# Column tiles of the input projection: split again at every use, or split once and reloaded as two parts

## The chip, the cores and the metric

The kernel runs on one core of a Trainium2 chip. The metric is the device time of one execution in microseconds (us), lower is better; given are the median and the extremes of three runs. A further execution was recorded by the hardware profiler; its own time stands beside its span in the table below. Engines are named as the profile names them: PE (TensorE; PEld its weight loads), DVE (VectorE), ACT (ScalarE), POOL (GpSimd), SP (SyncE, which here does nothing but issue DMAs).

## The reference, cut to what matters

One layer of a hybrid trunk over 2048 latent tokens (width 1024) and 256 context tokens, in float32:

- h = modulate(rmsnorm(x)); one projection p = h @ w_in, with w_in of 1024 x 3584. Its 28 column tiles of 128 are seven groups of four heads: forward gate (0 to 3), backward gate (4 to 7), v (8 to 11), q (12 to 15), output gate g (16 to 19), and u and v of a gated MLP (20 to 23, 24 to 27).
- The context uses the gates and v only (tiles 0 to 11), for the states in which the latent scans start.
- The first five groups feed a bidirectional gated linear recurrence with a 128 x 128 state per head; the last two feed a spatial gating unit over chunks of 128 positions.
- The outputs are joined and go through w_out, a residual add, a norm, a gated MLP with a 3x3 depthwise convolution, a residual add, and a last norm.

```python
q = split_heads(silu(p[..., 3*w:4*w]), HG_HEADS) * (HG_DIM ** -0.5)
o_f, h_f = chunk_gla(q, k_f, v, logf_f, h0_f)
o_b, h_b = chunk_gla(flip_t(q), flip_t(k_b), flip_t(v), flip_t(logf_b), h0_b)
```

## The kernel before, in words

**Products in three terms.** The operands go to TensorE in type f32r. A float32 operand a is split into hi = cast(a) and lo = a - hi, and a product is hi·hi + hi·lo + lo·hi. `split` (lines 117 to 120) issues the cast on ACT (L119) and the subtraction on DVE or POOL (L120). The transposed input is held as xh and xl, the context as ch and cl.

**The w_in stage.** The latent sequence is worked in two halves of 1024 tokens (hh = 0, 1), since xh and xl hold one half. A key is a column tile with a kind of input (context or latent). `run_banks` (L480 to L505) goes through a list of banks: 512 columns of the sequence (256 for the context), 24 matmuls each (8 slices of the contraction, three terms), after which a sink reads the PSUM bank. A latent key has two banks. In the first half the list mixes 12 context keys with 28 latent ones, in an order that is written out; the second half has 28 more, so there are 68 uses of 28 tiles. The two gate tiles of a head alternate bank by bank (forward, backward, forward, backward); otherwise a key's two banks follow each other.

**The column tiles.** `load_raw` (L199) loads a tile as 128 x 1024 float32 (512 KB, rows of 512 bytes in DRAM) into one of three raw buffers, which two background tasks share. `split_w` (L204) splits it into whi and wlo in one of two slots. `run_banks` splits the current key and the next one; a third is loaded ahead only around context keys. A slot is free when the last matmul of its old key is done; the cast waits for that. The subtraction runs on DVE for the first seven splits and then for the odd ones below 20, else on POOL.

**The recurrence.** `hg` (from L717) handles a head in steps: the sum of both keys (kd, L719, POOL), then seven levels. In each level TensorE makes score products (sc<-Q,K, eight chunks), DVE copies them by a mask (L745), multiplies the queries by totals of decay (`level_update`, L469), `level_keys` multiplies the keys, one half on DVE and the other on POOL (L544), with copies on ACT (L546), and `next_tot` (L471 to L477) makes the totals of the next level (L476). After the levels come transposes, state products, a chain and an output. In the second half `deferred` (from L819) finishes the first half's backward direction, with four loads.

**What sets the order.** The program is traced once. Steps of the recurrence (`hg_q`) and of background work (`bg_q`: x of the second half, the blocks of w_ada, w_out) are put between the matmuls of a bank by a running estimate of TensorE's time (`slot`); `later(fn, wait)` puts a function off by that many microseconds of the estimate. A scheduler then orders each engine's queue; instructions under `pin` keep the order of the trace. Each engine works its queue in order, SP too: an SP instruction that waits holds back all DMAs behind it.

**Other places the prediction names.** At the half turn, xh and xl are reloaded from DRAM in sixteen pieces of 512 KB (L992, L993). `w_out_ops` (L878 to L893) splits w_out in the first half and stores both parts in DRAM (wo_d, L891 and L892), from where 1 MB tiles are loaded at the end of the stage (L813). `x_start` loads, squares (L220) and transposes the first half of x beside the context keys. L639 is the gate product of the MLP heads on POOL (nt).

Of the kernel before, what the change touches and what calls it, by code (L numbers as in the profile page):

```python
# [9 lines left out]
F32 = mybir.dt.float32  # L10
F32R = mybir.dt.float32r
# [7 lines left out]
P = 128  # L19
D = 1024  # L20
NK = D // P
# [3 lines left out]
CTX = 256  # L25
# [8 lines left out]
AL = 512  # L34
# [38 lines left out]
def tile_trunk(ctx, tc, x, c, cx, c_ctx, w_ada, b_ada, norm_mix, norm_ffn, w_in, hg_norm, sgu_g, sgu_b,  # L73
               w_sp, b_sp, w_out, w_up, conv_w, conv_b, w_down, norm_final, masks, out):
    nc = tc.nc
    V, S, G, T = nc.vector, nc.scalar, nc.gpsimd, Tensor(nc.tensor)
    ld = nc.sync.dma_start
    st = nc.sync.dma_start
    pin = tc.keep_in_program_order
# [6 lines left out]
    dr = ctx.enter_context(tc.tile_pool(name="dr", bufs=1, space=DRAM))  # L86
# [30 lines left out]
    def split(hi, lo, raw, eng=None, keep=lambda i: i):  # L117

        keep(S.copy(hi, raw))  # L119
        (eng or G).tensor_sub(lo, raw, hi.bitcast(F32))  # L120
# [7 lines left out]
    class Pump:  # L128
# [22 lines left out]
        def slot(self):  # L151
            due = [fn for at, fn in self.soon if at <= T.t]
            self.soon = [e for e in self.soon if e[0] > T.t]
            for fn in due:
                fn()
            if self.tasks and T.t >= self.at:
                self.step()
# [11 lines left out]
    hg_q, bg_q = Pump(), Pump()  # L169
# [7 lines left out]
    with es1:  # L177
        ps = es1.enter_context(tc.tile_pool(name="ps1", bufs=1, space=PSUM, reuse_waits="tile"))
        p1 = es1.enter_context(tc.tile_pool(name="p1", bufs=1, reuse_waits="tile"))
# [11 lines left out]
        def bank(tag):  # L191
            return ps.tile([P, 512], F32, tag=tag, name=tag, bufs={"pj": 3, "sc": 2, "mi": 3}[tag])
# [1 line left out]
        def raw_tile():  # L194
            return p1.tile([P, D], F32, tag="raw", name="raw", bufs=3)

        w_n, w_raw, w_free = [0], {}, [0, 1]

        def load_raw(key):  # L199
            raw = raw_tile().rearrange("p (k c) -> p k c", c=P)  # L200
            ld(raw, w_in[:, key[0]:key[0] + P].rearrange("(k p) c -> p k c", p=P))
            w_raw[key] = raw

        def split_w(key, eng=None):  # L204
            if key not in w_raw:
                load_raw(key)
            raw, at = w_raw.pop(key), w_free.pop(0)
            hi = p1.tile([P, NK, P], F32R, tag=f"whi{at}", name="whi", align_bytes=AL)
            lo = p1.tile([P, NK, P], F32R, tag=f"wlo{at}", name="wlo", align_bytes=AL)
            w_n[0] += 1  # L210
            split(hi, lo, raw, eng or (V if w_n[0] < 8 or w_n[0] < 20 and w_n[0] % 2 else G))
            return hi, lo, at

        def x_sums():
# [30 lines left out]
        wts, rows, pa, nxt = {}, {}, {}, {}  # L245
# [53 lines left out]
        with tc.manual_schedule():  # L299
# [44 lines left out]
            for i in range(4):  # L344
                ld(xg[i], x_rows[i])
            ada_sums(6, 8)
            nxt[0, CTX] = split_w((0, CTX), G)
            ada_products(3, 1)
            pz = bank("pj")
# [6 lines left out]
            for k in range(4, NK):  # L356
                ctx_mod(k, V)
            nxt[HW, CTX] = split_w((HW, CTX), V)
        xl = p1.tile([P, NK, TH], F32R, tag="xl", name="xl", align_bytes=AL)
        xh = p1.tile([P, NK, TH], F32R, tag="xh", name="xh", align_bytes=AL)  # L360
# [110 lines left out]
        def next_tot(tot, W, B):  # L471
            nb = W // B
            od = B in (1, 4, 16, 64)
            t2 = ph.tile([P, 2 * (W // (2 if od else 4))], F32, tag=f"T{int(od)}", name="tot")
            t2 = t2[:, :nb].rearrange("p (d n) -> p d n", d=2)
            V.tensor_mul(t2, tot[:, :, 0::2], tot[:, :, 1::2])  # L476
            return t2  # L477


        def run_banks(banks, peek=None):  # L480

            keys = [(b[0], b[2]) for b in banks]
            tail = [(peek, 512)] if peek is not None else []
            for i, (col, n0, n, sink, pre) in enumerate(banks):
                if pre is not None:
                    pre()
                up = list(dict.fromkeys(keys[i:] + tail))
                for key in up[:2]:
                    if key not in nxt:
                        nxt[key] = split_w(key)  # L490
                if len(up) > 2 and up[2] not in w_raw and up[2] not in nxt and any(k[1] == CTX for k in up[:3]):
                    load_raw(up[2])
                hi, lo, at = nxt[keys[i]]
                hiT, loT = (chl, cll) if n == CTX else (xh, xl)
                pj = bank("pj")
                sl = slice(n0, n0 + n)
                for k in range(NK):
                    if k and n == 512:
                        slot()
                    T.matmul(pj[:, :n], hi[:, k, :], hiT[:, k, sl], start=(k == 0), stop=False)  # L500
                    T.matmul(pj[:, :n], hi[:, k, :], loT[:, k, sl], start=False, stop=False)
                    T.matmul(pj[:, :n], lo[:, k, :], hiT[:, k, sl], start=False, stop=(k == NK - 1))
                sink()(n0, n, pj[:, :n])
                slot()
                if keys[i] not in keys[i + 1:]:  # L505
                    w_free.append(nxt.pop(keys[i])[2])
# [57 lines left out]
        def ctx_state(h, F, K, vt):  # L564
            tot = F
            for B in LV:
                level_update(K, CTX, B, tot, True)
                tot = next_tot(tot, CTX, B)
            yield 9.5
            pt = bank("mi")  # L570
            for d in range(2):
                for i in range(2):
                    o = (2 * d + i) * P
                    T.transpose(pt[:, o:o + P], K[:, d, i * P:(i + 1) * P], ident)
            kt = ph.tile([P, 512], F32, tag="on", name="ckt", bufs=2)
            S.copy(kt, pt)
            yield 2.0
            pd = bank("mi")
            for d in range(2):
                for i in range(2):  # L580
                    o = (2 * d + i) * P
                    T.matmul(pd[:, o:o + P], kt[:, o:o + P], vt[:, i * P:(i + 1) * P], start=True, stop=True)
            for d, dst in ((0, hf[h]), (1, hb[h])):
                a, b = (0, 1) if d == 0 else (1, 0)
                t = ph.tile([P, P], F32, tag="cdh", name="cdh", bufs=2)
                S.copy(t, pd[:, (2 * d + a) * P:(2 * d + a + 1) * P])
                V.scalar_tensor_tensor(out=dst, in0=t, scalar=tot[:, 1 - d, b:b + 1],
                                       in1=pd[:, (2 * d + b) * P:(2 * d + b + 1) * P], op0=ALU.mult, op1=ALU.add)
            yield 0.0
# [19 lines left out]
        for h in range(NH):  # L609
            F, K, vt = sets[h % 2]  # L610

            def pre(h=h):
                if h >= 2:
                    need(hg_q, ("ctx", h - 2))
                if h:
                    F, K, vt = sets[(h - 1) % 2]
                    hg_q.add(marked(ctx_state(h - 1, F, K, vt), ("ctx", h - 1)))
# [99 lines left out]
        def hg(hh, h, F, K, qs, vt, sgt):  # L717
# [16 lines left out]
            for l, B in enumerate(LV):  # L734
                dims = [[2 * B, P // (2 * B)], [TH + B, 2], [1, B]]
                if B == 1:
                    dims = dims[:2]
                if B == P // 2:
                    dims = dims[1:]
                for g in range(0, NCH, 4):  # L740
                    pb = bank("sc")
                    for i in range(4):
                        off = (g + i) * P
                        T.matmul(pb[:, i * P:(i + 1) * P], K[:, 0, off:off + P], view(Q, off, dims), start=True, stop=True)
                    V.copy_predicated(sc[:, g:g + 4, :], view(msk, l * P, [[0, 4], [1, P]]),  # L745
                                      pb.rearrange("p (c t) -> p c t", t=P))
                level_update(Q, TH, B, tot, False)
                K = level_keys(K, B, tot)
                tot = next_tot(tot, TH, B)
                yield 4.2  # L750
# [227 lines left out]
        for item in "f1 v2 b1 f2 u2 b2 f3 v3 u3 b3".split():  # L978
# [8 lines left out]
            seq += with_post(part, post)  # L987
            post = nxt_post if item[0] == "b" else lambda: None
        run_banks(seq, 4 * HW)
        for q in range(0, TH, 512):  # L990
            for k in range(0, NK, 2):
# [37 lines left out]
        def wo_hook():  # L1029
# [3 lines left out]
            open_wo()  # L1033
        seq[i] = (*seq[i][:4], wo_hook)
        run_banks(seq)
        bg_q.drain()
        hg_q.flush()
# [29 lines left out]
    def c_tile():  # L1067
        return px.tile([P, NK, P], F32R, tag="fl", name="fl", bufs=2, align_bytes=AL)
# [50 lines left out]
    for n, u in enumerate(units):  # L1119
        at = first[n] if n < 2 else [14 * (n // 2) + 2 * i + 3 * (n % 2) for i in range(7)]  # L1120
# [307 lines left out]
    for n, (u, i) in enumerate(prods):  # L1428
# [5 lines left out]
        hi, lo = u.A[i]  # L1434
# [14 lines left out]
        if n == NP - 8:  # L1449
            g2.append(c_tile().rearrange("p a b -> p (a b)").bitcast(F32))  # L1450
            ld(g2[0], g_d[1:2, :].broadcast_to([P, D]))
            t = c_tile().rearrange("p a b -> p (a b)").bitcast(F32)
            for f in range(2):
                load_m(0, f, t[:, f * 512:f * 512 + 512])
        if n in (NP - 4, NP - 3, NP - 2):
            f = n - NP + 4
# [83 lines left out]
    for n in range(3, len(seq)):  # L1540
        tg, f = seq[n]
# [64 lines left out]
```

## Time and profile before

| | |
|---|---|
| time, median of 3 runs | 2584.08 us (2579.35 to 2584.96) |
| profiled execution, own time | 2583.23 us |
| its span | 2581.3 us |
| mean granted TensorE clock | 0.992 of full speed |
| w_in, raw loads | 68 of 512 KB |
| all DMA | 336.42 MB, mean 130 GB/s |
| HBM read, written | 236.69 MB, 97.59 MB |

The span runs from the first to the last instruction on record. A busy time is the time in which an engine had work; its share is that of the span. A row of a timeline gives start, duration, engine, line, operation, output <- inputs with shapes and, in brackets, how long the engine stood idle before it and what it then waited for. A group row gives the busy time of all, the mean of one in ns, and the idle time before them by releaser.

### The profile page before, as it was taken

The numbers are of one execution on the slowest core, as the hardware profiler recorded it, in microseconds if no ns is written. First come the engines' busy times: TensorE is split into PE (matmuls) and PEld (weight loads), VectorE is DVE, ScalarE is ACT, GpSimd is POOL, SyncE is SP. The second block draws the span as 40 slices with busy tenths as digits, with TensorE's granted clock in tenths as the row PEclk, the third lists the DMA queues.
The fourth block names the chain that finished last, engine by engine and source line by source line (L and its number), as shares of the span: only waits on it lengthen the run. The fifth ranks groups of instructions, "written<-read, shape, count | busy, mean of one in ns | idle before, by whom it ended". The sixth has DMA issues, their size and how long they took to land. (4 is left out here: it accounts for less than half of the span.)

```text
span 2581.3 us, 32786 instructions
## 1 busy us (share of the span) xinstructions
PE 2503.6 (97%) x12123; PEld 2066.2 (80%) x12123; DVE 1634.9 (63%) x2174; ACT 905.0 (35%) x1524; POOL 1052.7 (41%) x871
## 2 busy tenths in 40 slices
PE   7999999999999998999999999999999999999997
PEld 4787887888888887788788888788788888888886
DVE  5867784644555666466898778599999983212212
ACT  2554334333434332344433333333333332111111
POOL 1344232232243243002687887877877810000000
PEclk8999999999999999999999999999999999999999
DMA  8355445561022124668722222732222364313221
GB/s 286 105 193 163 145 123 196 184 209 58 30 86 82 43 84 163 212 208 273 243 88 95 77 92 89 268 125 90 88 89 89 101 204 128 114 45 114 73 90 67
DMA packets 282492, 336.42 MB, mean 130 GB/s; under 512 B 31057, under 2 KB 214089, under 8 KB 278621
## 3 DMA queue, kind: packets, MB, share of 16 engines
q1 hardware_dynamic: 279076, 333.59, 39.2%
q8 instruction: 96, 1.57, 0.2%
q10 hardware_dynamic: 3257, 0.75, 0.1%
q14 instruction: 63, 0.52, 0.1%
HBM read 236.69 MB, written 97.59 MB: 129 GB/s over the span
## 5 line engine op out<-in xcount | busy, mean ns | idle before, releaser
L1281 DVE SCALAR_TENSOR_TENSOR dn<-gp,taps,dn 128x1024 f32<-128x1024 f32 x352 | 448.0, 1279 | 20.6 <-ACT dn L1278 17.3
L120 POOL TENSOR_TENSOR Al<-raw,Ah 128x512 fp32r<-128x512 f32 x264 | 344.8, 1314 | 96.2 <-ACT Ah L119 88.4
L65 PE MATMUL pj<-xh,whi 128*128 128x512 f32 x896 | 364.9, 408 | 0.5 <-ACT xh L119 0.5
L65 PE MATMUL pj<-xl,whi 128*128 128x512 f32 x896 | 351.9, 393 | 1.8 <-DVE xl L120 1.1
L65 PE MATMUL pj<-xh,wlo 128*128 128x512 f32 x896 | 352.2, 393 | 1.0 <-DVE wlo L120 1.0
L65 PE MATMUL up<-xah,Al 128*128 128x512 f32 x704 | 275.8, 392 | 2.3 <-POOL Al L120 2.3
L65 PE MATMUL up<-xah,Ah 128*128 128x512 f32 x704 | 276.3, 393 | 1.7 <-ACT Ah L119 1.7
L65 PE MATMUL up<-yl,Ah 128*128 128x512 f32 x704 | 274.3, 390 | 3.2 <-DMA yl<-yd 3.1
L112 POOL TENSOR_SCALAR rs<-ss 128x1 f32<-128x1 f32 (+1 forms) x24 | 7.1, 297 | 642.0 <-DVE xt L1516 323.3
L119 ACT CAST Ah<-raw 128x512 fp32r<-128x512 f32 x265 | 161.1, 618 | 299.2 <-PE up L65 249.4
L120 DVE TENSOR_TENSOR ml<-mr,mh 128x512 fp32r<-128x512 f32 x85 | 58.7, 690 | 299.7 <-ACT mh L119 299.7
L120 POOL TENSOR_TENSOR wlo<-raw,whi 128x1024 fp32r<-128x1024 f32 x56 | 140.8, 2514 | 230.9 <-ACT whi L119 215.6
L65 PE MATMUL up<-yh,Ah 128*128 128x512 f32 x528 | 208.1, 395 | 0.0
L65 PE MATMUL up<-yh,Al 128*128 128x512 f32 x528 | 206.9, 392 | 0.0
L65 PE MATMUL up<-xal,Ah 128*128 128x512 f32 x528 | 205.5, 389 | 0.0
L65 PEld LDWEIGHTS pj<-xh,wlo 128*128 128x128 f32 x896 | 169.0, 189 | 37.3 <-DVE wlo L120 1.7
L65 PEld LDWEIGHTS pj<-xh,whi 128*128 128x128 f32 x896 | 169.6, 189 | 34.3 <-issue 3.5
L65 PEld LDWEIGHTS pj<-xl,whi 128*128 128x128 f32 x896 | 169.6, 189 | 33.5 <-DVE xl L120 2.1
L65 PE MATMUL dn<-wo,o 128*128 128x512 f32 x768 | 184.9, 397 | 3.7 <-DMA wo<-wo_d 2.2
L65 PE MATMUL dn<-wh,ml 128*128 128x512 f32 x480 | 186.8, 389 | 0.0
L65 PE MATMUL dn<-wl,mh 128*128 128x512 f32 x480 | 186.8, 389 | 0.0
L65 PE MATMUL dn<-wh,mh 128*128 128x512 f32 x480 | 186.7, 389 | 0.0
(307 smaller groups left out, 4941.2 us busy)
## 6 DMA issues: line engine op xcount, KB each, us to landing
raw<-in_w_up_dram SPq DMA_DIRECT2D x88, 512.0 KB
raw<-in_w_in_dram SPq DMA_DIRECT2D x68, 512.0 KB
mr<-m SPq DMA_DIRECT2D x85, 256.0 KB
raw<-in_w_ada_dram SPq DMA_DIRECT2D x32, 512.0 KB
m<-cv SPq DMA_DIRECT2D x22, 544.0 KB
m<-cv SPq DMA_DIRECT2D x22, 480.0 KB
xt<-in_w_down_dram SPq DMA_DIRECT2D x19, 512.0 KB
wa<-in_w_ada_dram SPq DMA_DIRECT2D x8, 1024.0 KB
```

What stands on the lines that cost most here:

```text
L65: return self.engine.matmul(out, lhsT, rhs, **kw)
L112: keep(G.tensor_scalar(out=r[:, :n], in0=ss, scalar1=scale, scalar2=bias, op0=ALU.mult, op1=ALU.add))
L119: keep(S.copy(hi, raw))
L120: (eng or G).tensor_sub(lo, raw, hi.bitcast(F32))
L1281: V.scalar_tensor_tensor(out=cr, in0=gt[:, t // 3:t // 3 + RH, t % 3:t % 3 + GW], scalar=taps[:, t * NF + f:t * NF + f + 1], in1=cr, op0=A ...
```

## The change

One tile of two parts takes the place of whi and wlo in each slot. The first use of a column loads and splits as before, and then stores both parts (1 MB) in a DRAM tensor of its own; the store is put off by 1.0 us of the estimate. Every later use, 40 of the 68, loads the 1 MB into the slot by one DMA on SP, with no cast and no subtraction. The load ahead of a third key is left out where that key's column is stored already. The counter that picks DVE or POOL now counts real splits alone. The product in `next_tot` is pinned.

In the built program there are 28 raw loads of 512 KB, 28 stores and 40 loads of 1 MB in place of 68 raw loads. ACT has 40 casts fewer and POOL 40 subtractions fewer; DVE keeps 12 subtractions. The matmuls are the same, and TensorE's order is the same but for the start, where transposes of x stand ahead of three context columns that they followed before. The first matmul and the cast of a column wait for the slot's old readers; where the slot's old content was a first use, its store is one of these.

```diff
-        w_n, w_raw, w_free = [0], {}, [0, 1]
+        w_n, w_raw, w_free, w_d = [0], {}, [0, 1], {}
...
         def split_w(key, eng=None):
+
+            at = w_free.pop(0)
+            t = p1.tile([P, 2, NK, P], F32R, tag=f"w{at}", name="w", align_bytes=AL)
+            hi, lo = t[:, 0], t[:, 1]
+            col = key[0] // P
+            if col in w_d:
+                ld(t.bitcast(F32), w_d[col])
+                return hi, lo, at
             if key not in w_raw:
                 load_raw(key)
-            raw, at = w_raw.pop(key), w_free.pop(0)
-            hi = p1.tile([P, NK, P], F32R, tag=f"whi{at}", name="whi", align_bytes=AL)
-            lo = p1.tile([P, NK, P], F32R, tag=f"wlo{at}", name="wlo", align_bytes=AL)
             w_n[0] += 1
-            split(hi, lo, raw, eng or (V if w_n[0] < 8 or w_n[0] < 20 and w_n[0] % 2 else G))
+            split(hi, lo, w_raw.pop(key), eng or (V if w_n[0] < 8 or w_n[0] < 20 and w_n[0] % 2 else G))
+            w_d[col] = dr.tile([P, 2, NK, P], F32, name=f"wi{col}")
+            hg_q.later(lambda: st(w_d[col], t.bitcast(F32)), 1.0)
             return hi, lo, at
...
-            V.tensor_mul(t2, tot[:, :, 0::2], tot[:, :, 1::2])
+            pin(V.tensor_mul(t2, tot[:, :, 0::2], tot[:, :, 1::2]))
...
-                if len(up) > 2 and up[2] not in w_raw and up[2] not in nxt and any(k[1] == CTX for k in up[:3]):
+                if (len(up) > 2 and up[2] not in w_raw and up[2] not in nxt and any(k[1] == CTX for k in up[:3])
+                        and up[2][0] // P not in w_d):
                     load_raw(up[2])
```

## The prediction

> **What bounds the kernel now.** I read the page first, then busy time by stretch, the groups by form and the single waits of TensorE. Page:
>
> ```profile
> span 2581.3 us, 32786 instructions
> PE 2503.6 (97%) x12123; PEld 2066.2 (80%) x12123; DVE 1634.9 (63%) x2174; ACT 905.0 (35%) x1524; POOL 1052.7 (41%) x871
> ```
>
> TensorE is busy 97% of the span, so only time in which it stands still can be won. The view by stretch (columns: us, busy time of each engine, clock, DMA share, GB/s), cut at the end of the start, at the half turn and at the end of the w_in stage:
>
> ```profile
> 0.00:100.00 100.00, 79.01 (x394) 52.11 (x395) 66.07 (x108) 38.09 (x71) 27.41 (x28) 0.93 0.62 213
> 100.00:542.00 442.00, 425.69 (x2321) 360.17 (x2321) 293.13 (x463) 184.99 (x292) 147.68 (x105) 0.99 0.53 172
> 542.00:1026.00 484.00, 470.16 (x2699) 406.75 (x2697) 285.12 (x445) 182.57 (x372) 167.12 (x117) 1.00 0.24 80
> 1026.00:2581.30 1555.30, 1528.73 (x6712) 1247.13 (x6712) 990.63 (x1159) 499.36 (x790) 710.48 (x622) 1.00 0.39 129
> ```
>
> The change lies wholly before 1026. What follows is bound by TensorE (1528.73 of 1555.30), and nothing in it is edited, so a gain or loss before 1026 moves the end one for one. TensorE stands still 442 - 425.69 = 16.3 us between 100 and 542 and 484 - 470.16 = 13.8 us after that: 30 us at most, in which the removed work has only a part. The groups by form (busy, mean ns, idle before and its releasers):
>
> ```profile
> L120 POOL TENSOR_TENSOR wlo<-raw,whi 128x1024 fp32r<-128x1024 f32 x56 | 140.8, 2514 | 230.9 <-ACT whi L119 215.6 <-DMA xh<-xh_d 12.0 <-PE sc L65 3.0
> L65 PE MATMUL sc<-Q,K 128*128 128x128 f32 x896 | 121.0, 290 | 15.0 <-DVE Q L469 8.7 <-ACT sc L730 4.4 <-ACT K L546 1.9
> L119 ACT CAST whi<-raw 128x1024 fp32r<-128x1024 f32 x68 | 71.3, 1048 | 113.0 <-PE pj L65 82.7 <-issue 23.0 <-DMA raw<-in_w_in_dram 7.3
> L476 DVE TENSOR_TENSOR tot<-tot 128x512 f32<-128x512 f32 x8 | 5.5, 688 | 0.2
> ```
>
> The split does not stand in a TensorE row; it is the recurrence's score products (sc<-Q,K) that wait, for VectorE or ScalarE. The question is which of those waits stand behind a split.
>
> **What the change removes.** Of 68 uses of a column 28 are first ones; 40 casts (40 x 1.048 = 42 us of ScalarE) and 40 subtractions (40 x 2.514 = 101 us of GpSimd) go: 12 in the first half, where a context column is used again, and all 28 in the second. VectorE keeps its 12. I looked at each TensorE wait for a removed split just ahead of it. The clearest case (start, us, engine, work, idle before):
>
> ```profile
> 861.52 2.40 POOL L120 TENSOR_TENSOR wlo<-raw,whi 128x1024 fp32r<-128x1024 f32 x1 [4.83 <-ACT whi L119]
> 863.88 2.23 POOL L544 TENSOR_TENSOR K<-K,tot 128x512 f32<-128x512 f32 x1
> 866.14 0.62 ACT L546 COPY K<-K 128x512 f32<-128x512 f32 x1 [3.69 <-POOL K L544]
> 866.81 2.97 PE L65 MATMUL sc<-Q,K 128*128 128x128 f32 x15 [1.93 <-ACT K L546]
> ```
>
> GpSimd does the subtraction, then the key product that ScalarE's copy and TensorE wait for. Without the 2.40 us the product ends that much earlier and 1.93 us go. A second place, with VectorE in it:
>
> ```profile
> 972.63 2.40 POOL L120 TENSOR_TENSOR wlo<-raw,whi 128x1024 fp32r<-128x1024 f32 x1
> 974.99 2.25 POOL L639 TENSOR_TENSOR nt<-nt,gu 128x512 f32<-128x512 f32 x1
> 973.62 2.49 DVE L469 TENSOR_TENSOR Q<-Q,tot 128x1024 f32<-128x1024 f32 x1
> 976.03 1.75 DVE L544 TENSOR_TENSOR K<-K,tot 128x512 f32<-128x512 f32 x1
> 980.01 1.20 DVE L469 TENSOR_TENSOR Q<-Q,tot 128x1024 f32<-128x1024 f32 x1
> 976.25 2.02 PE L65 MATMUL sc<-Q,K 128*128 128x128 f32 x16 [1.25 <-DVE Q L469]
> 981.36 1.91 PE L65 MATMUL sc<-Q,K 128*128 128x128 f32 x15 [0.99 <-DVE Q L469]
> ```
>
> The same VectorE product takes 2.49 us beside the subtraction and 1.20 us alone: 1.29 us longer, and TensorE waits 1.25 us for it. Four smaller waits follow a removed subtraction by a few microseconds; at 339.60 the producer (kd) is GpSimd's own next instruction:
>
> ```profile
> 333.83 2.40 POOL L120 TENSOR_TENSOR wlo<-raw,whi 128x1024 fp32r<-128x1024 f32 x1 [5.21 <-ACT whi L119]
> 339.60 1.60 PE L65 MATMUL sc<-qs,kd 128*128 128x128 f32 x12 [0.89 <-POOL kd L719]
> 435.82 1.38 PE L65 MATMUL sc<-qs,kd 128*128 128x128 f32 x10 [0.77 <-POOL kd L719]
> 781.19 2.02 PE L65 MATMUL sc<-Q,K 128*128 128x128 f32 x16 [0.72 <-DVE Q L469]
> 786.23 2.02 PE L65 MATMUL sc<-Q,K 128*128 128x128 f32 x16 [0.94 <-DVE Q L469]
> ```
>
> Sum: 1.93 + 1.25 + 0.99 + 0.89 + 0.77 + 0.72 + 0.94 = **7.5 us**. I take all of it: some of these will find another late producer, but VectorE products are also stretched where TensorE has slack, and that relief I count at nothing. The ends are 1.93 + 0.89 + 0.77 = 3.6 us (only where GpSimd is itself the late producer) and 10 us (two more such waits that I leave out).
>
> The Trainium skill ("SBUF — State Buffer", section "SBUF: two separate sides") says that a GpSimd operation and a VectorE operation with two SBUF inputs hold one port pair in turn, each for its whole length. The 2.49 us agree: the product ends 1.08 us after the subtraction does (973.62 + 2.49 against 972.63 + 2.40). But by that rule the gate product (nt), moved up into the subtraction's place, would block the query product just as long, the 1.25 us would stay, and the sum would be 6.2 us.
>
> **What the change adds: loads.** Each of the 40 later uses issues one 1 MB load on SP, into the slot itself, so it can't start before TensorE's last product from the slot's old column. Before, the 512 KB raw load came earlier and only cast and subtraction (1.05 + 2.51 = 3.6 us) followed the release. For a load, from issue to the cast that waited for it (other waits of this kind: 3.8 and 4.1 us):
>
> ```profile
> 360.73 0.37 SPq L201 DMA_DIRECT2D raw<-in_w_in_dram  x1
> 364.47 1.05 ACT L119 CAST whi<-raw 128x1024 fp32r<-128x1024 f32 x1 [1.14 <-DMA raw<-in_w_in_dram]
> 542.00:552.00 10.00, 10.00 (x53) 8.54 (x52) 6.29 (x2) 3.72 (x4) 6.56 (x3) 1.00 1.05 401
> ```
>
> 512 KB took 3.74 us. At the 401 GB/s of the last row, with the DMA engines full, 0.52 MB are 1.3 us, so about 2.4 us are fixed; 1 MB is then 2.4 + 2.6 = 5.0 us (estimate; between 3.7, were size free, and 7.5, twice the row). A load is hidden where the slot is free for longer. A bank of 24 products takes about 5.4 us (520.27 to 525.72 below), and a slot rests for the banks of the other column: for most loads two of them and products of the recurrence, 9 us or more. Six slots rest for a single bank, 5.2 to 6.2 us. At four of them the load is about as long as the rest, 0 to 0.5 us late each: **+0.5 us** in all (0 to 2). The two others cost more.
>
> The first is released at 520.5, in the last gate pair of the first half, whose load stands in SP's order behind two stores of w_out:
>
> ```profile
> 520.41 0.33 SPq L891 DMA_DIRECT2D wo_d<-wo_hi  x1
> 521.27 0.46 SPq L892 DMA_DIRECT2D wo_d<-raw  x1
> 520.27 0.39 PE L65 MATMUL pj<-xh,whi 128*128 128x512 f32 x1
> 525.72 0.39 PE L65 MATMUL pj<-xh,whi 128*128 128x512 f32 x1
> ```
>
> Issued at 522 it lands at 527, against the first use at 525.7: **+1.3 us** (0 to 2.5).
>
> The second is the half turn, where sixteen 512 KB pieces of x come back:
>
> ```profile
> 529.00 0.38 SPq L993 DMA_DIRECT2D xl<-xl_d  x1
> 542.64 0.46 SPq L993 DMA_DIRECT2D xl<-xl_d  x1
> 551.23 0.48 PE L65 MATMUL pj<-xh,whi 128*128 128x512 f32 x1
> ```
>
> 8.4 MB at 401 GB/s take 21 us, from 529.5 to 550.5; the last piece is needed at 551.2, so the reload is only just hidden. The changed order puts the 1 MB of the next column in the middle of it, ahead of the last nine pieces: everything behind lands 2.6 us later and the last pieces miss their products by 1 to 2 us, and the column after that follows at 543, lands at 556 and is wanted at about 555. I take **+2.6 us** (0.6 to 4.5).
>
> **What it adds: stores.** Each of the 28 first uses stores 1 MB, and the slot's next column may not be written until that store is done. No row shows a store of this size; I take the load's 5.0 us, between 2.5 and 10. In most of the stage a slot is read for 10 us or more, and the store hides behind those reads. At the start it can't: context columns are 256 wide, used up in 3 us. Casts there, and TensorE's waits between 40 and 110:
>
> ```profile
> 55.73 1.05 ACT L119 CAST whi<-raw 128x1024 fp32r<-128x1024 f32 x1 [1.79 <-PE pj L65]
> 63.09 1.05 ACT L119 CAST whi<-raw 128x1024 fp32r<-128x1024 f32 x1 [2.33 <-PE pj L65]
> 68.77 1.05 ACT L119 CAST whi<-raw 128x1024 fp32r<-128x1024 f32 x1 [1.72 <-PE pj L65]
> PE pj L65 <- DVE wlo L120: 1.8, 2, 1.0
> ```
>
> These slots are now written again as soon as TensorE lets go. The column cast at 49.1 has its subtraction done by 51.4, its store done at 56.8, and so the cast of 55.73 comes 1 us late; in the same way the two others come some 1.5 us late, and more if the x rows issued on SP in between share the engines. Behind a waiting cast ScalarE holds the squares of x and the casts of x, for which VectorE and then TensorE's x transposes wait. Against that, the changed order moves transposes of x ahead of three of these columns, and TensorE has slack here (79 of the first 100 us). I take **+1.5 us**, from -1 to +8, near the cheap end because the first links come out at 1 to 1.5.
>
> **Neither.** 48 MB more pass the DMA engines, at shares of 0.53 and 0.24: nothing outside the places named. The pinned product of totals moves behind the key product at one level of each head (8 x 0.688 us, quoted above); VectorE does the same work, and the total is next read a level later: nothing, between -3 and +3. Raw loads ahead are left out only for columns already stored. The 28 stores are queued on SP, each waiting there for its subtraction, with raw and x loads behind it; outside the start these have slack.
>
> **Sum:** -7.5 + 0.5 + 1.3 + 2.6 + 1.5 = -1.6 us. The profiled execution took 2583.23 (2581.3 of span and 1.9 around it), so 2581.6; against the median of 2584.08, 0.85 above it, it is 2582.5. I say **2582**, between the two.
>
> **The rivals.** *Stores set the pace at the start (slower).* Place: columns four to eight, 50 to 90 us. Price: if a store with x rows beside it takes 8 us instead of 5, a slot turns in about 11 us, two slots give a column every 5.5 us, TensorE needs one each 3, and four columns lose 2.5 us each: +10 in place of +1.5, so 2590 to 2592. It decides from a store of 6 us on. For it: VectorE's wait rows and the 0.62 DMA share of the first 100 us; against it: the moved transposes. The Trainium skill ("DMA: Bandwidth & Descriptors", "Anatomy of one DMA — SWDGE (gpsimd) path") says that completion waits for the write's receipt, longest where the target is HBM; it speaks of another queue kind, and no row here shows it.
>
> *Full relief (faster).* The scores find no other late producer, stretched VectorE work gives more (10 us), and loads and start cost 1 to 2: 2574 to 2576. For it: TensorE stands still 30 us, mostly behind VectorE and ScalarE. Against: the gate product at 974.99.
>
> *It does nothing.* The waits stay because another producer is as late, and the loads hide: 2583 to 2584. For it: most waits are under 1 us.
>
> **How the numbers follow.** Forecast (2577 to 2586) 0.40, stores at the start 0.27, full relief 0.23, nothing 0.10. About 0.2% (5.2 us) is what a measurement of this kernel can tell from no change. Faster by more: 0.23 and a quarter of the forecast, 0.33; slower: the stores and a tenth of the forecast, 0.31; the rest, 0.36, within. Range: 2573 to 2593, from full relief to the stores' price with a late half turn.
>
> **What would show it.** The waits at 866.8 and 339.6 gone, POOL down by about 100 us and ScalarE by 42; TensorE waiting for a w load at the half turn and at 525, 1 to 3 us each; casts of the first columns 1 to 2 us later, TensorE reaching the first 512-wide banks within 2 us of before. I am wrong if TensorE waits for w loads in quiet stretches too (a load above 6 us), or if its arrival at 110 is late by over 4 us.

## The result

| | median of 5 runs | lowest to highest |
|---|---|---|
| before | 2582.16 us | 2579.35 to 2584.96 |
| after | 2592.74 us | 2590.17 to 2595.31 |

The ratio is 1.004, 95% interval 1.0026 to 1.0054: the change costs about 10.6 us. The forecast was 2582 with a range to 2593; the rival in which the stores set the pace at the start named 2590 to 2592. One execution of e8_turn below (2781.07 us) fell in a slower state of the chip and is left out of its figures.

The profiled execution of after took 2590.17 us, the fastest of its five, so the two traces show only 7 of the 10.6 us. The view by stretch of after, in the columns used for before (busy times of TensorE, its weight loads, VectorE, ScalarE, GpSimd; clock, DMA share, GB/s):

```profile
0.00:100.00 100.00, 72.28 (x343) 47.96 (x344) 58.93 (x93) 34.43 (x64) 22.17 (x27) 0.88 0.85 290
100.00:542.00 442.00, 428.83 (x2347) 363.91 (x2346) 288.33 (x477) 175.50 (x284) 115.05 (x94) 0.99 0.67 228
542.00:1026.00 484.00, 470.23 (x2703) 406.74 (x2703) 252.16 (x439) 159.32 (x346) 93.09 (x87) 1.00 0.32 113
```

GpSimd is relieved as forecast (147.68 to 115.05 and 167.12 to 93.09 us). But TensorE does 7 us less in the first 100 us, at a DMA share of 0.85 in place of 0.62. The most useful reading is the lag of each bank: the start of its first product, after less before. Banks are counted in the order of the trace. This table is worked out from the TensorE rows (24 products a bank), in us:

```
stretch                                     lag before it, after it    step
start (bank 0 to 17)                            -1.4      10.9        +12.3
rest of the first half (17 to 66)               10.9       5.9         -5.0
half turn (66 to 74)                             5.9       8.9         +2.9
second half (74 to 122)                          8.9       4.7         -4.1
w_out and later (122 to the last product)        4.7       7.2         +2.5
```

The last row isn't the change's: nothing is edited there, the step falls at waits for other loads, and other kernels below move by -2.1 to +4.2 in that stretch. The -5.0 isn't either, or not by itself: three kernels below, without a single store (e1_pin, e12_tile) or with four that gain nothing (e13_other4), win 2.6, 5.4 and 3.3 us in that stretch against this same recorded execution of before. A profile of this kernel is thus good to some 4 us in the first half; what is under that is read here from neighbouring kernels.

At the start, the single waits of TensorE between 40 and 115, first of before, then of after (us in total, times, longest):

```profile
PE pj L65 <- DVE wlo L120: 1.8, 2, 1.0
PE mi L69 <- DVE xfl L231: 1.6, 2, 0.8
PE mi L69 <- DVE xg L226: 1.5, 2, 1.2
```

```profile
PE pj L65 <- ACT w L119: 5.3, 1, 5.3
PE mi L69 <- DVE xk L233: 3.1, 1, 3.1
PE mi L69 <- DVE xg L233: 3.0, 3, 2.5
PE mi L69 <- DVE xfl L238: 1.4, 1, 1.4
```

TensorE waits for a cast of a column (5.3 us at once) and for the scaled rows of x (xg, xk). Why is that cast late? ScalarE's rows, of before and then of after:

```profile
59.71 1.05 ACT L119 CAST whi<-raw 128x1024 fp32r<-128x1024 f32 x1
64.90 0.37 ACT L559 COPY cb<-mi 128x256 f32<-128x256 f32 x1 [0.21 <-PE mi L69]
```

```profile
63.52 0.37 ACT L567 COPY cb<-mi 128x256 f32<-128x256 f32 x1 [4.90 <-PE mi L69]
71.55 1.98 ACT L119 CAST w<-raw 128x1024 fp32r<-128x1024 f32 x2
```

The cast of the fifth column ran at 59.71, ahead of a copy in the context's part of the recurrence (cb). In after it stands behind that copy, which waits 4.9 us for transposes on TensorE, and behind casts and squares of x; it runs at 71.55 with no idle time of its own ahead of it. It did not wait for a store: none of ScalarE's waits between 40 and 110 is put down to one. With the store in the program, the scheduler has put the cast later in ScalarE's queue and transposes of x earlier in TensorE's, and so each of the two engines holds at its head what waits for the other.

Not all of the 12.3 us is standing still. Worked out from the TensorE rows between banks 0 and 17, the idle time grows by 8.2 us, and the same 538 instructions are busy for 95.0 us in place of 90.8. The granted clock was lower in these 60 us (the number after the five busy times; the next is the DMA share), first of before, then of after, then of e2b_order below:

```profile
40.00:100.00 60.00, 52.67 (x320) 45.27 (x321) 46.71 (x79) 31.72 (x60) 17.80 (x12) 0.90 0.39 119
```

```profile
40.00:100.00 60.00, 46.16 (x264) 40.79 (x265) 39.21 (x63) 28.07 (x53) 12.57 (x11) 0.80 0.81 259
```

```profile
40.00:100.00 60.00, 48.34 (x251) 42.98 (x251) 39.47 (x63) 28.00 (x53) 12.20 (x11) 0.73 0.39 123
```

No run here shows why the clock was lower where TensorE stood still more.

### The profile page after: what moved, and what is told of

Read it like the earlier page. It is cut to its first block, busy times and chain, and to the rows that moved or that the text cites. A ratio compares the mean times of both kernels' runs of the same rounds, so it can differ in the third digit from the quotient of the medians.

```text
span 2588.4 us, 32721 instructions
## 1 busy us (share of the span) xinstructions
PE 2507.3 (97%) x12123; PEld 2071.9 (80%) x12123; DVE 1591.5 (61%) x2174; ACT 868.5 (34%) x1484; POOL 942.7 (36%) x831
## 5 line engine op out<-in xcount | busy, mean ns | idle before, releaser
L65 PE MATMUL pj<-xh,w 128*128 128x512 f32 x1792 | 599.6, 402 | 5.3 <-DMA w<-wi 3.0
L65 PEld LDWEIGHTS pj<-xh,w 128*128 128x128 f32 x1792 | 337.8, 189 | 76.2 <-issue 3.7
L65 PE MATMUL pj<-xl,w 128*128 128x512 f32 x896 | 353.2, 394 | 0.6 <-POOL xl L120 0.5
L65 PEld LDWEIGHTS pj<-xl,w 128*128 128x128 f32 x896 | 170.1, 190 | 31.2 <-POOL xl L120 1.0
L65 PEld LDWEIGHTS dn<-wo,o 128*128 128x128 f32 x768 | 142.8, 189 | 32.3 <-DMA wo<-wo_d 1.7
L119 ACT CAST mh<-mr 128x512 fp32r<-128x512 f32 x85 | 52.8, 621 | 329.0 <-PE dn L65 305.5
L65 PEld LDWEIGHTS up<-xah,Al 128*128 128x128 f32 x704 | 133.0, 189 | 33.2 <-POOL Al L120 3.9
```

The source lines that it names most:

```text
L65: return self.engine.matmul(out, lhsT, rhs, **kw)
```

## The experiments

Each is given with its edit against the changed kernel, unless another is named.

### e1_pin: the pinned product alone

```diff
-            V.tensor_mul(t2, tot[:, :, 0::2], tot[:, :, 1::2])
+            pin(V.tensor_mul(t2, tot[:, :, 0::2], tot[:, :, 1::2]))
```

The edit is made to the kernel before.

> The kernel before with the product of decay totals pinned, and nothing else of the change. Both theories (the stores at the start cost the time; the loads cost it) expect no difference: within 2 us of the kernel before.

Measured: 2579.97 us beside 2581.74, ratio 0.9996 (0.9987 to 1.0005). The pin is no part of the loss.

### e2_ctx: no stores of context columns

```diff
+            if key[1] == CTX:
+                return hi, lo, at
             w_d[col] = dr.tile([P, 2, NK, P], F32, name=f"wi{col}")
```

> The changed kernel, but context uses are split without a store; a column is stored at its first latent use. So 40 splits, 28 stores, 28 loads, all loads in the second half. If the stores at the start cost the time: the lag of about 12 us that TensorE has by bank 17 (measured 10.9 behind, 12.3 with the head start that it had) is gone, within 1.5 us of before; the second half still loses 3 us at the half turn and wins about 4 after it; the first half wins nothing, so 2580 to 2583 in all. If the loads cost the time: at least 2588.

Measured: 2597.48 beside 2581.74, ratio 1.0052 (1.0038 to 1.0065). Before bank 17 this leaves 4 stores, of latent columns, of the 13 in after. The first part came as expected: from bank 0 to 17 the lag grows by 2.1 us instead of 12.3. The total did not: the first half then loses 8.2 us between banks 17 and 66. So stores cost time beyond the start as well, which neither theory had. The largest single wait of SP between 110 and 545, of this kernel (L220 is the store) and of the kernel before (us in total, times, longest):

```profile
SPq L220 <- POOL w L120: 75.4, 17, 12.2
```

```profile
SPq L855 <- DVE acc L857: 42.8, 16, 5.3
```

A store waits at the head of SP's queue until GpSimd has done the subtraction, and loads of x and of w_out wait behind it. Raw columns come late too. ScalarE's casts wait for them between 165 and 545, first in e2_ctx, then in e12_tile, which has no store (11.9 us in e6_pool, 7.3 in the kernel before):

```profile
ACT w L119 <- DMA raw<-in_w_in_dram: 19.9, 7, 7.5
```

```profile
ACT w L119 <- DMA raw<-in_w_in_dram: 3.2, 5, 1.2
```

### e2b_order: the order of the changed kernel, without stores of context columns

```diff
+                hold = pin if i < 8 else lambda x: x
-                    T.matmul(pj[:, :n], hi[:, k, :], hiT[:, k, sl], start=(k == 0), stop=False)
+                    hold(T.matmul(pj[:, :n], hi[:, k, :], hiT[:, k, sl], start=(k == 0), stop=False))
```

This is e2_ctx with the products of the first eight banks (all three terms) and the casts of context columns pinned.

> As e2_ctx, with the matmuls of the first eight banks and the casts of context columns pinned to the order of the trace: TensorE's order at the start is then that of the changed kernel, without a store there. If TensorE really waits for the stores, the start is within 2 us of before. If the order of the queues alone makes the lag (transposes of x ahead of three columns, casts of columns behind casts of x), TensorE is 8 to 12 us late at bank 17 here too, and the time is about 2591.

Measured: 2608.56 beside 2581.74, ratio 1.0104 (1.009 to 1.0118). At bank 17 it is 12.2 us late, 12.7 from bank 0. Its first store, of a latent column, is issued at 80.62; by then, at bank 5 (76.1), 8.2 of the 12.7 us are lost, and e2_ctx issues such a store at 74.99 and has no lag. Its ScalarE rows show the same kind of knot, with the fifth column's cast (66.90) fewer places back than in after:

```profile
65.58 0.37 ACT L571 COPY cb<-mi 128x256 f32<-128x256 f32 x1 [5.51 <-PE mi L69]
65.85 1.14 ACT L119 CAST xh<-xfl 128x512 fp32r<-128x512 f32 x2
66.90 1.05 ACT L119 CAST w<-raw 128x1024 fp32r<-128x1024 f32 x1
```

So a lag as long comes from order alone, with no context column stored. It is made up differently: 5.2 us more of standing still and 7.6 of longer instructions, at a clock of 0.73. TensorE waits for the scaled rows of x as in after (xk and xg, 7.5 us in all against 6.1), at a DMA share of 0.39, so crowded DMA engines are not needed for that; its wait for the column's cast is 2.1 us against 5.3. (The list of banks is run twice, so the pins hold the first eight banks of the second half too; what this kernel loses there is not the change's.)

### e5_stores: stores, but no loads

```diff
-            if col in w_d:
-                ld(t.bitcast(F32), w_d[col])
-                return hi, lo, at
```

A column stored already is split again and not stored again; the load ahead is as before.

> The changed kernel with its 28 stores, but no loads: every use splits from the raw column as before. If the stores at the start cost the time: TensorE is about 11 us late at bank 17 as in the changed kernel, no loss at the half turn, no gain in the second half, so 2592 to 2595. If the loads cost the time: within 3 us of before.

Measured: 2608.47 beside 2581.74, ratio 1.0103 (1.0089 to 1.0117). From bank 0 to 17 it loses 13.0 us, and from 17 to 66 another 4.0 where the changed kernel won 5.0. Against the expectation it also loses 2.8 us at the half turn, without a load there: the reload of x is issued 19.9 us later, 3.4 more than its lag at bank 66, and TensorE waits 1.5 us for xl. It wins nothing after that, as expected (it loses 2.9). The stores alone cost about 27 us, more than either theory said; with the 40 loads the kernel is some 16 us faster than without them.

### e6_pool and e6_act: the stores off SP's queue

```diff
-            hg_q.later(lambda: st(w_d[col], t.bitcast(F32)), 1.0)
+            hg_q.later(lambda: G.dma_start(w_d[col], t.bitcast(F32)), 1.0)
```

Both are made to e2_ctx; e6_act has S.dma_start and 4.0.

> As e2_ctx, with the 28 stores issued by GpSimd, where most of the subtractions run, in place of SP. If what costs the first half there (9.9 us late at bank 62, none at bank 25) is that a store waits on SP for its subtraction (75 us of such waits) and holds back the loads of x and w_out behind it: at bank 62 within 3 us of before, and 5 to 8 us less than e2_ctx in all. If it is the traffic of the stores on the DMA engines: at bank 62 still 8 us or more late.

> As e6_pool, but the stores are issued by ScalarE, put off by 4 us instead of 1. SP's queue is free of them here too: the theory of SP's queue expects the first half as in e6_pool or up to 4 us worse, where ScalarE waits for a subtraction; the theory of traffic expects 8 us or more late at bank 62.

Measured: e6_pool 2596.06 (ratio 1.006, 1.0047 to 1.0074) and e6_act 2604.13 (1.0089, 1.0075 to 1.0103), both beside 2580.64. My theory of SP's queue fell as the whole account. In e6_pool one of its steps is gone, at bank 27, where e2_ctx has loads of x behind a store (a step of 7.0 us there, 0.7 here); but other steps come, and at bank 66 it is 12.8 us late; e6_act is 23.7 us late there. At bank 62, where the theory of traffic expected 8 us or more, they are 12.5 and 18.7 us late, so that theory stands.

### e8_turn and e9_tight: without the loads that have no time

```diff
-            if key[1] == CTX:
+            if key[1] == CTX or col in (16, 8, 17, 18, 19, 25):
                 return hi, lo, at
```

e9_tight against e6_pool; e8_turn names only 16 and 8. The columns named are never stored: e8_turn has 26 stores and e9_tight 22.

> As e6_pool, and the two columns that the second half begins with (16 and 8) are split again there in place of a 1 MB load in the middle of the reload of x. If that load makes the loss at the half turn (3 to 4 us between banks 66 and 74): at most 0.5 us there, and 3 us less than e6_pool in all. If the loss is in the score products, moved by the scheduler: it stays.

> As e8_turn, and also columns 17, 18, 19 and 25, whose slots rest for a single bank, are split again in the second half. If those loads come too late (in the changed kernel 1.5, 0.6 and 1.5 us at banks 90, 102 and 112): no step there, 1 to 3 us less than e8_turn, and the second half wins 6 us; in all 2576 to 2580. If four more subtractions on GpSimd cost as much as they save: the same as e8_turn.

Measured: e8_turn 2590.25 (ratio 1.0033, 1.0019 to 1.0046) and e9_tight 2587.5 (1.0026, 1.0017 to 1.0035; 2576 to 2580 was expected), beside 2580.64. The half turn (banks 66 to 74) costs 2.5 us in e6_pool and nothing in e8_turn. But in after TensorE waits there for no load. These are all its named waits between 535 and 600 (before has none until its bank 74, at 589):

```profile
PE sc L65 <- DVE Q L476: 1.9, 1, 1.9
PE pj L65 <- ACT F L528: 0.6, 1, 0.6
```

Two groups of score products stand ahead of bank 70, whose first product they followed before, and one of them waits there for VectorE's queries (sc<-Q). In e8_turn both are back in their old place. So the two loads make the loss, but by the order that comes with them. In the second half of after, the three tight loads do show by name, here the first and the last:

```profile
729.02 0.47 PE L65 MATMUL pj<-xh,w 128*128 128x512 f32 x1 [1.36 <-DMA w<-wi]
916.61 0.50 PE L65 MATMUL pj<-xh,w 128*128 128x512 f32 x1 [1.24 <-DMA w<-wi]
```

The first of these loads is issued at 721.32 and the last at 909.39, so 7.7 and 7.2 us pass to the product that waits, where I had taken 5.0 for a load.

In e9_tight no wait for a load is left in the second half, and it wins 7.9 us from bank 74 to 122 (e8_turn 3.3). What remains is the first half, and not all of it is in the trace: e9_tight's recorded execution (2581.83 us) is the fastest of its eleven, 5.7 us below their median. The largest step in it, 6 us at bank 54; SP, ScalarE and TensorE of e9_tight:

```profile
422.98 0.33 SPq L895 DMA_DIRECT2D raw<-in_w_out_dram  x1
427.71 0.62 ACT L119 CAST wo_hi<-raw 128x512 fp32r<-128x512 f32 x1 [9.37 <-DVE raw L899]
429.59 1.08 ACT L119 CAST w<-raw 128x1024 fp32r<-128x1024 f32 x1
430.72 0.80 PE L65 MATMUL pj<-xh,w 128*128 128x512 f32 x1 [6.04 <-ACT w L119]
```

and ScalarE before:

```profile
421.99 1.05 ACT L119 CAST whi<-raw 128x1024 fp32r<-128x1024 f32 x1 [1.98 <-issue]
429.38 0.62 ACT L119 CAST wo_hi<-raw 128x512 fp32r<-128x512 f32 x1 [4.83 <-DVE raw L889]
```

The column's cast stood ahead of a cast of w_out before and stands behind one here, which waits through VectorE for a w_out load issued at 422.98. It is the knot of the start once more, between other engines. Bank 55 adds 5.0 us, and by bank 57 all but 4.4 of the two steps is won back; what is lost after that was not followed.

### e11_traffic: the traffic without the dependences

```diff
+            col = key[0] // P
+            if col not in w_d:
+                w_d[col] = dr.tile([256, D], F32, name=f"wi{col}")
+                hg_q.later(lambda: st(w_d[col], w_out[:256, :]), 1.0)
```

The kernel before, after its split.

> The kernel before, splitting at every use, with 28 copies of 1 MB from one DRAM tensor to another added, issued on SP at the trace points of the stores. They wait for no subtraction and hold no slot, but load the DMA engines as the stores do, and the scheduler counts them. If the traffic of the stores or its place in the scheduler's account costs the first half: 8 us or more late at bank 66. If it is the waits that a store brings (SP for the subtraction, the cast for the slot) and the order that the scheduler makes of these: at most 3 us late at bank 66, and 2580 to 2585.

Measured: 2600.57 beside 2580.17, ratio 1.0076 (1.0062 to 1.0091): 18.3 us late at bank 66, against my expectation. But all of it is there by bank 17 (5.7 us up to bank 15, then a TensorE wait of 10 us for a column's cast). The copies wait for nothing and so run early, all 28 of them by 161.2 us, when bank 17 is about to start (161.9):

```profile
L215 SPq DMA_DIRECT2D wi<-in_w_out_dram x28: 494/588/4172, 30.7 to 161.2; - x28
```

In the first 100 us its DMA share is 0.94:

```profile
0.00:100.00 100.00, 78.60 (x377) 53.68 (x378) 64.25 (x103) 37.55 (x71) 24.23 (x28) 0.88 0.94 339
```

So traffic can cost time at the start. Of the rest of the first half the run says nothing: there its DMA share is 0.52 (165 to 542), as before (0.54), against 0.67 in e2_ctx and 0.64 in e9_tight. Whether traffic makes the loss of these kernels between banks 17 and 66 is not tested.

### e10_four, e12_tile, e13_other4: how many loads the gain needs

```diff
-            if key[1] == CTX:
+            if key[1] == CTX or col not in (6, 7, 21, 23):
                 return hi, lo, at
```

e10_four against e2_ctx. e13_other4 has (12, 13, 14, 20) there; e12_tile stores nothing and loads nothing.

> As e2_ctx (stores on SP), but only columns 6, 7, 21 and 23 are stored, at their first latent use, and loaded in the second half: 4 stores, 4 loads, 64 splits. These are the four whose second split stands ahead of the steps that the second half gains in e9_tight (1.3 us by bank 100, 2.9 by 110, 1.2 by 114, 1.6 by 122). If single waits behind single splits make the gain, and the cost lies in the number of stores: the second half gains 5 to 7 us between banks 74 and 123, the first loses at most 3, and the time is 2574 to 2579, below the kernel before. If the gain needs GpSimd and ScalarE relieved as a whole: at most 2 us gained, 2580 to 2584.

> The one tile of two parts and the pinned product, every use split, no store and no load: e10_four without its four stores and loads. If the 5.5 us that e10_four wins in the first half come from the tile (the scheduler frees a slot's two parts together and orders differently), it wins them here too, and the second half is as before (within 1 us between banks 74 and 123): 2573 to 2577. If they come from the four stores and loads: within 2 us of before.

> As e10_four, but with four other columns (12, 13, 14 and 20), whose second splits no TensorE wait follows. If single waits behind single splits make the gain of the second half: at most 1 us between banks 74 and 123, where e10_four won 6.5. If four subtractions fewer on GpSimd are the gain, wherever they are: 4 us or more there.

Measured: e10_four 2569.35 beside 2580.17, **ratio 0.9957 (0.9943 to 0.997), faster than both kernels**; e12_tile 2579.23 (0.9994, 0.9985 to 1.0003) and e13_other4 2580.85 (1.0003, 0.9994 to 1.0012) beside 2580.7, both no different from before. From bank 74 to 122 e10_four wins 6.5 us, e12_tile loses 1.4, e13_other4 loses 1.6. Four loads in the right places win what forty won, and four in other places nothing. (e10_four's recorded execution is the slowest of its six, which lie between 2563.5 and 2575.49.) Of the 5.5 us that e10_four's trace wins in the first half, e12_tile's has as much, and its median doesn't show it: so I put that down to the recorded execution of before. The waits of the score products on the queries from 600 to 1026, first of e12_tile, then of e10_four:

```profile
PE sc L65 <- DVE Q L474: 6.3, 5, 2.1
```

```profile
PE sc L65 <- DVE Q L478: 2.1, 4, 0.7
```

4.2 of the roughly 8 us between the two are these named waits; the rest is spread over idle times that are too small to be named, and e10_four's median is lower by 10.8 us than before, of which its trace shows 8.

## Why the prediction was wrong

**The gain (-7.5 us): mechanism right, size about right.** The second half was to win 1.93 + 1.25 + 0.99 + 0.72 + 0.94 = 5.8 us. In after, the falls of the lag between banks 74 and 122 add up to 8.1, against which stand 3.6 for the tight loads; e9_tight wins 7.9 and e10_four 6.5, and the pair of e10_four and e13_other4 shows that it takes the right columns. The places agree only roughly: the falls are 1.3 at bank 99, 2.9 at 109 and 1.7 at 121, where 1.66, 1.93 and 2.24 were forecast, and 1.2 at 114, where nothing was. Of the 2.9 at 109, e12_tile has 1.5 with every column split. The two waits of the first half can't be told from the scatter of the profiles there.

The rule of the Trainium skill ("SBUF — State Buffer", "SBUF: two separate sides") by which the gate product would block the query product just as long, so that 1.25 us stay, did not come out so. In e10_four:

```profile
962.45 1.29 POOL L649 TENSOR_TENSOR nt<-nt,gu 128x512 f32<-128x512 f32 x1
963.44 1.38 DVE L478 TENSOR_TENSOR Q<-Q,tot 128x1024 f32<-128x1024 f32 x1
963.71 2.08 POOL L554 TENSOR_TENSOR K<-K,tot 128x512 f32<-128x512 f32 x1
```

Moved up, the gate product takes 1.29 us in place of 2.25 and is nearly done when the query product starts; that one takes 1.38, and the key product on GpSimd, which starts just behind it, takes 2.08. That agrees with the Trainium skill's own words in that section, that the first to start holds the ports; I had applied the rule with the gate product's stretched duration. Nor is it the missing subtraction that moves the gate product up: in e12_tile, which splits this column too, it also stands ahead of the subtraction (966.98, 1.30 us), so the place comes with the new order of the queues.

**Loads: +0.5, +1.3 and +2.6.** The half turn was +2.6 and measured 2.9 in after, 2.5 to 4.2 in its neighbours, none in e8_turn. That the size agrees is luck: the forecast had TensorE wait for the last pieces of x and for a column's load, and it waits for neither, but 2.5 us for VectorE and ScalarE in a changed order. The load at 520.5 cost nothing (the lag is 5.9 at banks 64, 65 and 66). The tight loads were undersized: 1.5 + 0.6 + 1.5 = 3.6 us in after, at three of the four places, each behind the loads that finish a head of the first half; from issue to the waiting product they take 6.7 to 7.7 us and not 5.0. Together 6.5 against 4.4.

**Stores at the start (+1.5): the step that failed.** It should have been 12. I worked out when a slot would be free and found casts 1 to 1.5 us late. That was the store's effect on the chip, and no wait of that kind is in the trace there (in the whole stage casts wait 1.4 us for stores). What came is in the built order, which I had and did not cost: transposes of x ahead of three columns I put down *for* the change, as if an earlier transpose were an earlier result. TensorE then stood behind x rows that weren't there, and ScalarE's queue, whose order I had not followed, held the column's cast behind a copy that needed those transposes. The rival had the place right and the price nearly so (+10, 2590 to 2592), and the reason wrong: it decided by the time of a store, while e2b_order has a lag as long with no context column stored, and e2_ctx, without these stores, has none. What the forecast also lacked is the clock: 4.1 of the 12.3 us are the same instructions taking longer at a granted clock of 0.80 in place of 0.90. Whether in after the crowded DMA engines add to the lag (e11_traffic lost 5.7 us there) is not separated.

**Stores elsewhere ("these have slack"): failed too.** With 22 to 28 stores in the first half and no loads there (e2_ctx, e6_pool, e6_act, e8_turn, e9_tight) it loses 5.9 to 16.1 us between banks 17 and 66, where e12_tile without stores wins 5.4. In after the twelve loads of that half make up for its stores there: it wins 5.0 where e5_stores, without loads, loses 4.0. SP's queue is not the cause by itself (e6_pool, e6_act). In the one step that I followed it is again the order of casts in ScalarE's queue; the cause of the rest stays open, the traffic of the stores included.

**The pin: 0, as forecast** (e1_pin).

## What to carry to other kernels

Where a scheduler lays out in-order queues, a new dependence is paid first in the order of every queue near it: compare that order on all engines, and for each instruction that moved ask what it now stands behind and what that waits for. A transfer that nothing on the path needs (here 24 of 28 stores and 36 of 40 loads) is still a cost; find the few places where the removed work ends a wait and change only those. Read a loss by its lag along the path, against several neighbouring kernels, before any theory. And see in its trace that a control runs where it was meant to run: the copies of e11_traffic, freed of every wait, had all run ahead of the stretch that they were to test.

## What the runs showed of the hardware

The landing of a 1 MB store, which no row of before showed, is given in the list of DMA issues of e6_pool, where GpSimd issues it (the last number is the median in us from issue to landing; for stores issued on SP the list gives none):

```profile
wi<-w POOLq DMA_DIRECT2D x28, 1024.0 KB, 6.6
```

I had taken 5.0. The DRAM to DRAM copies of 1 MB in e11_traffic filled the DMA engines to a share of 0.94 in the first 100 us, against 0.62 before. TensorE's granted clock between 40 and 100 us was 0.90 in before, 0.80 in after and 0.73 in e2b_order. And the recorded executions of one unedited stretch, from the last bank to the end, differ by up to 6 us from kernel to kernel.
